# Gate and up projections of a SwiGLU layer as seven block products instead of eight

## The chip, the cores and the metric

The kernel runs on one core of one Trainium2 chip. The metric is the device time of one execution in microseconds (us). Several engines of the core work side by side, each through a queue of its own in order: TensorE (PE, matmuls; its weight loads are listed apart as PEld), VectorE (DVE), ScalarE (ACT), GpSimd (POOL) and SyncE (SP), which issues the transfers.

## The reference

A trunk of two layers on 512 tokens of 1024 features, in float32. Each layer runs a SwiGLU sub-layer, a mixer (convolution and attention) and a second SwiGLU sub-layer, so the program has four SwiGLU stages. The change concerns the first two products of this line:

```python
def _swiglu(h, w_gate, w_up, w_down):
    return (jax.nn.silu(h @ w_gate) * (h @ w_up)) @ w_down
...
h = _rmsnorm(x, norm_g[l, 0]) * (1.0 + mod[:, 0, 1]) + mod[:, 0, 0]
x = x + 0.5 * mod[:, 0, 2] * _swiglu(h, ffn_w_gate[l, 0], ffn_w_up[l, 0], ffn_w_down[l, 0])
```

`h` is 512 x 1024, `w_gate` and `w_up` are 1024 x 2816, `w_down` is 2816 x 1024. The vectors `mod` (shift, scale and gate of each sub-layer) are products of a conditioning vector with a large matrix `ada_w`.

## The kernel before

Activations lie transposed, features on the 128 partitions and the 512 tokens along the row, so a matmul has a 128 x 128 weight block as the loaded operand and up to 512 tokens as the moving one. To keep float32 accuracy each operand is split into a rounded part `hi` and a rest `lo`, and `step` issues three matmuls for one product: hi·hi, hi·lo and lo·hi (lines 216, 217, 218). The two parts of a weight are made on the chip: `Unit.split` has ScalarE cast a piece of 128 x 512 (line 195) and VectorE subtract the cast from the original (line 196). `hh` and `hl` hold the two parts of `h`.

The 2816 hidden features are 22 blocks of 128. `ffn` walks through them in parts of 6, 6, 4, 3 and 3 blocks (`FF_PARTS`). `up` computes for each block m gate and up, 8 feature blocks each, 512 tokens at a time, 48 matmuls in all; `swiglu` then makes silu(gate)·up and splits it (lines 520 to 524). `down_part` multiplies the part's blocks with `w_down` and adds into the residual stream `xT` (line 377). The stages are joined by `boundary`, which ends the old stage with matmuls 256 tokens wide, normalises each half of the tokens as soon as it is there (`modulated`, lines 366 to 371 and 127) and does the first gate and up blocks of the next stage (m = 0 and 1, in the very first stage 0, 1 and 2) with matmuls 256 tokens wide.

Work that is not urgent is woven in: every second `step` calls `tick`, and at a rate of so many steps per tick a generator computes the `mod` vectors on VectorE, mostly with one weighted sum of 128 x 512 a step (line 292), after a transfer of 256 KB each. Such a vector takes 22 steps. Slots for parts (`R`), slots for float32 rows (`F`), four `raw` weight buffers of 128 x 2048 and eight banks of accumulators limit how far the engines run ahead of one another. The order on each engine is set when the program is built.

## Time and profile before

| what | value |
|---|---|
| median of 3 runs | 2733.66 us (2731.41 to 2736.07) |
| profiled execution, device time | 2730.47 us |
| its span, first to last instruction | 2728.5 us |
| TensorE, busy share of the span | 99% |
| VectorE, busy share | 55% |
| ScalarE, busy share | 37% |
| GpSimd, busy share | 11% |

The span lies 2.0 us under the device time of the same execution, and that time 3.2 us under the median. A busy share is an average over all stages; what an edit is worth is read from the stage that it lies in. Matmuls overlap in the profile, so what one costs is read from the distance between starts and not from its own duration.

### The profile page before, as it was taken

How to read it: one execution, taken by the hardware profiler on the slowest of the kernel's cores; microseconds unless marked ns; L12 is line 12 of the kernel's file. 1: busy time of each engine (PE TensorE's matmuls, PEld its weight loads, DVE VectorE, ACT ScalarE, POOL GpSimd, SP SyncE). 2: the span in 40 equal slices, each digit the busy share in tenths (PEclk: the TensorE clock that was granted, in tenths of full speed). 3: DMA queues.
4: the chain of work that ended last, by engine and by line, in shares of the span. 5: the costliest groups of instructions: out<-in, count | busy, mean ns of one | idle time of the engine just before them, and what ended most of it. 6: DMA issues, size and time to landing. Idle time of an engine off the chain costs nothing.

```text
span 2728.5 us, 35693 instructions
## 1 busy us (share of the span) xinstructions
PE 2690.2 (99%) x13489; PEld 2270.8 (83%) x13489; DVE 1513.6 (55%) x2718; ACT 1015.8 (37%) x2106; POOL 294.7 (11%) x887
## 2 busy tenths in 40 slices
PE   6999999999999999999999999999999999999998
PEld 5888789888888888888898888988888888988887
DVE  7955447664563468654485443756646534843434
ACT  4333236344352353332343232443444433532322
POOL 4100014111100020000030000311111000200001
PEclk8999999999999999999999999999999999999999
DMA  8843234342212247433374332333422322532321
GB/s 248 297 149 120 74 122 129 102 132 86 93 62 93 85 148 262 135 99 102 97 233 138 95 108 93 122 90 104 143 74 70 123 78 87 165 108 89 108 70 39
DMA packets 318104, 325.60 MB, mean 119 GB/s; under 512 B 10097, under 2 KB 281836, under 8 KB 317932
## 3 DMA queue, kind: packets, MB, share of 16 engines
q1 hardware_dynamic: 317604, 323.19, 37.1%
q8 instruction: 106, 1.74, 0.3%
q14 instruction: 66, 0.54, 0.1%
q10 hardware_dynamic: 328, 0.13, 0.0%
HBM read 321.15 MB, written 2.13 MB: 118 GB/s over the span
## 4 chain that ended last, share of the span: by engine, by line
PE 95%; DVE 2%; POOL 1%; ACT 1%; DMA 0%; issue 0%; ACTq 0%; DVEq 0%; POOLq 0%
PE mm L216 19%; PE mm L218 19%; PE mm L217 19%; PE o L216 5%; PE o L218 5%; PE o L217 5%; PE at L216 5%; PE at L218 5%; PE at L217 4%; PE mm L886 3%; PE o L733 2%; PE at L624 1%; PE at L626 1%; PE at L625 1%; PE at L400 0%; PE at L709 0%
## 5 line engine op out<-in xcount | busy, mean ns | idle before, releaser
L195 ACT CAST slots_r<-raw 128x512 fp32r<-128x512 f32 (+2 forms) x896 | 522.5, 595 | 1090.6 <-PE mm L217 658.5
L196 DVE TENSOR_TENSOR slots_r<-raw,slots_r 128x512 fp32r<-128x512 f32 (+1 forms) x890 | 573.2, 659 | 588.6 <-ACT slots_r L195 572.0
L216 PE MATMUL mm<-hh,slots_r 128*128 128x512 f32 (+1 forms) x1944 | 732.9, 377 | 0.0
L218 PE MATMUL mm<-hh,slots_r 128*128 128x512 f32 (+1 forms) x1944 | 726.7, 374 | 0.0
L217 PE MATMUL mm<-hl,slots_r 128*128 128x512 f32 (+1 forms) x1944 | 724.9, 373 | 0.0
L218 PEld LDWEIGHTS mm<-hh,slots_r 128*128 128x128 f32 x1944 | 365.2, 188 | 70.3
L217 PEld LDWEIGHTS mm<-hl,slots_r 128*128 128x128 f32 x1944 | 365.9, 188 | 62.4
L216 PEld LDWEIGHTS mm<-hh,slots_r 128*128 128x128 f32 x1944 | 365.9, 188 | 60.7 <-issue 0.6
L216 PE MATMUL mm<-slots_r 128*128 128x512 f32 (+1 forms) x584 | 212.3, 364 | 0.0
L218 PE MATMUL mm<-slots_r 128*128 128x512 f32 (+1 forms) x584 | 211.8, 364 | 0.0
L217 PE MATMUL mm<-slots_r 128*128 128x512 f32 (+1 forms) x584 | 211.8, 363 | 0.0
L292 DVE SCALAR_TENSOR_TENSOR slots_f<-slots_f,cs 128x512 f32<-128x512 f32 (+1 forms) x272 | 191.7, 721 | 18.7 <-DMA slots_f<-in_ada_w_dram 16.5
L391 POOL TENSOR_TENSOR slots_f<-slots_f 128x256 f32<-128x256 f32 x60 | 45.1, 752 | 1053.4 <-ACT slots_f L388 1047.6
L216 PE MATMUL o<-hh,slots_r 128*128 128x512 f32 x344 | 135.5, 394 | 0.0
L218 PE MATMUL o<-hh,slots_r 128*128 128x512 f32 x344 | 134.9, 392 | 0.0
L217 PE MATMUL o<-hl,slots_r 128*128 128x512 f32 x344 | 133.9, 389 | 0.0
L216 PE MATMUL o<-slots_r 128*128 128x512 f32 (+1 forms) x364 | 127.7, 351 | 0.6 <-ACT slots_r L523 0.6
L217 PE MATMUL o<-slots_r 128*128 128x512 f32 (+1 forms) x364 | 126.4, 347 | 0.2 <-DVE slots_r L127 0.2
L218 PE MATMUL o<-slots_r 128*128 128x512 f32 (+1 forms) x364 | 126.5, 348 | 0.0
L216 PE MATMUL at<-hh,slots_r 128*128 128x512 f32 x320 | 125.8, 393 | 0.0
L218 PE MATMUL at<-hh,slots_r 128*128 128x512 f32 x320 | 125.4, 392 | 0.0
L216 PEld LDWEIGHTS mm<-slots_r 128*128 128x128 f32 x584 | 110.2, 189 | 18.1 <-ACT slots_r L195 0.6
(179 smaller groups left out, 3762.8 us busy)
## 6 DMA issues: line engine op xcount, KB each, us to landing
slots_f<-in_ada_w_dram SPq DMA_DIRECT2D x256, 256.0 KB, 3.7
raw<-in_w_in_dram SPq DMA_DIRECT2D x52, 1024.0 KB, 5.1
raw<-in_ffn_w_gate_dram SPq DMA_DIRECT2D x42, 1024.0 KB, 5.3
raw<-in_ffn_w_up_dram SPq DMA_DIRECT2D x42, 1024.0 KB, 5.2
raw<-in_ffn_w_down_dram SPq DMA_DIRECT2D x32, 768.0 KB, 5.5
raw<-in_w_in_dram SPq DMA_DIRECT2D x48, 512.0 KB, 5.2
raw<-in_ffn_w_down_dram SPq DMA_DIRECT2D x20, 512.0 KB, 3.4
slots_f<-in_ada_w_dram SPq DMA_DIRECT2D x16, 512.0 KB, 7.3
```

The costliest lines, as they stand in the source:

```text
L195: A.copy(hv, src)
L196: (eng or V).tensor_tensor(lv, src, f(hv), op=ALU.subtract)
L216: T.matmul(dst, hi, xh[:, cols], start=first, stop=False)
L217: T.matmul(dst, hi, xl[:, cols], start=False, stop=False)
L218: T.matmul(dst, lo, xh[:, cols], start=False, stop=last)
L292: V.scalar_tensor_tensor(acc, w, cs[:, k:k + 1], acc, op0=ALU.mult, op1=ALU.add)
L391: G.tensor_tensor(acc, acc, sq, op=ALU.add)
L624: T.matmul(dst, qh[:, qs], kh[:, :, ks], start=True, stop=False)
L625: T.matmul(dst, qh[:, qs], kl[:, :, ks], start=False, stop=False)
L626: T.matmul(dst, ql[:, qs], kh[:, :, ks], start=False, stop=True)
L733: T.matmul(dst, a, b, start=first[bk], stop=True, skip_group_check=True)
L886: T.matmul(dst, a, b, start=k == 0 and r % 2 == 0 and n == 0, stop=True, skip_group_check=True)
```

## The change

Two blocks (m, m+1) of gate and up are now computed together, as a 2 x 2 product of blocks. The tokens are cut into halves, the 1024 features into halves, and the columns are "256 of gate" and "256 of up". Call the weight blocks a, c (gate, lower and upper features) and b, d (up). Plainly that is eight products of blocks, four for gate and four for up. `seven` forms sums of weight blocks (b-a, d-(b-a), d-b and c-(d-(b-a)), line 585 of the changed kernel), sums of blocks of `h` once per stage (`Sums`, lines 522 to 528), and gets the same four results from seven products (`product`), adding them up in accumulator banks and in float32 slots (lines 581 and 588). Each product takes a weight of 512 x 256 and 256 tokens: 24 matmuls of 256 columns. Its split is one cast and one subtraction of 128 x 1024 each (lines 549 and 146).

Ten pairs a stage go this way, nine in the first, where block 3 is still computed plainly: 39 pairs in the program. The rate of the `mod` steps is multiplied by 0.5 during `up` and by 2.2 during `down_part`. The first product of a pair is put into the pair before. The unsplit `h` is kept in 8 float32 slots (`whole`) until the sums are made; in the first stage it is put together again from its two parts (`rejoined`). `R` grows from 36 to 49 slots, of which 16 hold the sums, `F` shrinks from 25 to 19, and the mixer splits each convolution row where it is made instead of all eight in one place.

```diff
-N_R, N_F, RAWS = 36, 25, 4
+N_R, N_LOW, N_F, RAWS = 49, 33, 19, 4
+SHARE_UP, SHARE_DOWN = 0.5, 2.2
...
-            modulating["due"] += modulating["rate"]
+            modulating["due"] += modulating["rate"] * modulating["share"]
...
+    class Sums:
+        def __init__(self, whole):
+            self.slot = R.at(N_LOW, N_R - N_LOW)
...
+            h11, h21 = whole[:, :4, HALF[0]], whole[:, :4, HALF[1]]
+            h12, h22 = whole[:, 4:, HALF[0]], whole[:, 4:, HALF[1]]
+            V.tensor_tensor(h22, h21, h22, op=ALU.add)
+            self.split(0, h22)
+            V.tensor_tensor(h21, h11, h21, op=ALU.subtract)
+            V.tensor_tensor(h22, h22, h11, op=ALU.subtract)
+            self.split(1, h22)
+            self.split(2, h21)
+            V.tensor_tensor(h22, h12, h22, op=ALU.subtract)
+            self.split(3, h22)
+
+        def split(self, i, src):
+            A.copy(self.hi[:, i], src)
+            sub(self.lo[:, i], src, f(self.hi[:, i]))
...
+    def product(src, x, bank_, first=False):
+
+        hi, lo = R.take(2), R.take(2)
+        hv, lv = (s.ap.rearrange("p (k m) -> p k m", k=4) for s in (hi, lo))
+        A.copy(hv, src)
+        sub(lv, src, f(hv))
+        yield
+        for k in range(4):
+            xh, xl = x(k)
+            for i in range(2):
+                c_ = slice(i * P, (i + 1) * P)
+                dst = bank_[:, HALF[i]]
+                for n, (a, b) in enumerate(((hv[:, k, c_], xh), (hv[:, k, c_], xl), (lv[:, k, c_], xh))):
+                    T.matmul(dst, a, b, start=first and k == i == n == 0, stop=True, skip_group_check=True)
+            if k % 2:
+                tick()
...
+        one = bank("mm")
+        end(run(a, quarter(0, 0), one, True))
+        p1 = kept(one)
+        yield
+        minus(a, b, a)
+        three = bank("o")
+        p = run(a, sums(1), three, True)
+        minus(a, d, a)
+        end(p)
+        end(run(a, sums(2), one))
+        u2 = kept(one)
+        two = bank("at")
+        end(run(c, quarter(1, 0), two, True))
+        plus(p1, two)
+        minus(b, d, b)
+        end(run(b, sums(3), one))
+        u3 = kept(one)
+        plus(u3, three)
+        yield
+        minus(c, c, a)
+        end(run(c, quarter(1, 1), one))
+        end(run(d, sums(4), three))
+        plus(u2, three)
+        done(p1, u2, one, u3)
...
         def up(part):
+            modulating["share"] = SHARE_UP
...
+                pair = ahead.pop(m)
+                next(pair)
+                begin(m + 2)
+                for _ in pair:
+                    pass
...
         def down_part(part):
+            modulating["share"] = SHARE_DOWN
...
                 V.tensor_tensor(conv[m + i].ap, conv[m + i].ap, pd, op=ALU.mult)
+                conv[m + i] = split(conv[m + i])
...
-        zz = [split(s) for s in conv]
+        zz = conv
```

How the order on the engines moves is shown at three places. The first is TensorE inside `up`, far from the edges of a stage. Before, every matmul there runs over 512 columns, into one bank for eight feature blocks:

```order
L216 MATMUL at<-hh,slots_r 128x512
L217 MATMUL at<-hl,slots_r 128x512
L218 MATMUL at<-hh,slots_r 128x512
L216 MATMUL at<-hh,slots_r 128x512
L217 MATMUL at<-hl,slots_r 128x512
L218 MATMUL at<-hh,slots_r 128x512
```

In the changed kernel the same place reads as follows; `o` is the bank called three, `mm` one, `at` two, and 48 matmuls in a row are the last product of a pair and the second of the next:

```order
L558 MATMUL o<-slots_r 128x256 x48
L558 MATMUL mm<-slots_r 128x256 x24
L558 MATMUL at<-hh,slots_r 128x256
L558 MATMUL at<-hl,slots_r 128x256
L558 MATMUL at<-hh,slots_r 128x256 x2
L558 MATMUL at<-hl,slots_r 128x256
```

What moved: 96 matmuls of 512 columns a pair have become 168 of 256, and between two products on the bank `mm` a product on another bank stands.

The second place is VectorE at the start of the second SwiGLU stage (the second one of layer 0), where the sums of blocks of `h` are made. Before, the queue there holds the splits of the first weights, mod steps (L292) and the first two swiglu blocks:

```order
L292 SCALAR_TENSOR_TENSOR slots_f<-slots_f,cs 128x512
L281 TENSOR_TENSOR mod_8222<-dot,vec 128x4
L521 TENSOR_TENSOR slots_f<-slots_f,mm 128x512 x2
L196 TENSOR_TENSOR slots_r<-raw,slots_r 128x512
L127 TENSOR_TENSOR slots_r<-slots_f,slots_r 128x512 x2
L196 TENSOR_TENSOR slots_r<-raw,slots_r 128x512 x3
```

Now, right behind the first two sums (L522, L524), two mod steps and the split of the first product's weight, it holds these (L146 from `raw` is the split of a weight, from `slots_f` 128x1024 that of a sum, L585 a sum of weight blocks, L655 the swiglu of a plain block):

```order
L146 TENSOR_TENSOR slots_r<-slots_f,slots_r 128x1024
L585 TENSOR_TENSOR raw<-raw 128x1024
L525 TENSOR_TENSOR slots_f<-slots_f 128x4x256
L585 TENSOR_TENSOR raw<-raw 128x1024
L146 TENSOR_TENSOR slots_r<-raw,slots_r 128x1024
L146 TENSOR_TENSOR slots_r<-slots_f,slots_r 128x1024 x2
L528 TENSOR_TENSOR slots_f<-slots_f 128x4x256
L655 TENSOR_TENSOR slots_f<-slots_f,mm 128x512 x2
L146 TENSOR_TENSOR slots_r<-slots_f,slots_r 128x1024
L146 TENSOR_TENSOR slots_r<-slots_f,slots_r 128x512 x2
L585 TENSOR_TENSOR raw<-raw 128x1024
L146 TENSOR_TENSOR slots_r<-raw,slots_r 128x1024 x3
```

What moved: the split of the third product's weight (the first of the last three) stands behind sums, splits of sums and the two plain blocks.

The third place is VectorE inside `up`, in the same stage. Before, between two swiglu blocks there are four splits of 128x512 and mod steps:

```order
L196 TENSOR_TENSOR slots_r<-raw,slots_r 128x512 x4
L521 TENSOR_TENSOR slots_f<-slots_f,mm 128x512
L196 TENSOR_TENSOR slots_r<-raw,slots_r 128x512
L127 TENSOR_TENSOR slots_r<-slots_f,slots_r 128x512
L196 TENSOR_TENSOR slots_r<-raw,slots_r 128x512 x2
L521 TENSOR_TENSOR slots_f<-slots_f,at 128x512
```

Now the queue near the end of a pair reads (L588 adds a bank to a kept result, L670 and L666 are the two multiplications of swiglu):

```order
L146 TENSOR_TENSOR slots_r<-raw,slots_r 128x1024 x2
L588 TENSOR_TENSOR slots_f<-slots_f,o 128x512
L585 TENSOR_TENSOR raw<-raw 128x1024 x2
L146 TENSOR_TENSOR slots_r<-raw,slots_r 128x1024 x2
L670 TENSOR_TENSOR slots_f<-slots_f 128x512
L146 TENSOR_TENSOR slots_r<-raw,slots_r 128x1024
L146 TENSOR_TENSOR slots_r<-slots_f,slots_r 128x2x256
L146 TENSOR_TENSOR slots_r<-raw,slots_r 128x1024
L588 TENSOR_TENSOR slots_f<-slots_f,o 128x512
L585 TENSOR_TENSOR raw<-raw 128x1024
L666 TENSOR_TENSOR slots_f<-slots_f 128x512
```

What moved: additions that read a bank (L588) stand in the same queue ahead of splits for products that TensorE will need next.

## Rows read from the trace of the kernel before

**Rows 1.** Head of the page: span, then busy time and share of each engine.

```profile
span 2728.5 us, 35693 instructions
PE 2690.2 (99%) x13489; PEld 2270.8 (83%) x13489; DVE 1513.6 (55%) x2718; ACT 1015.8 (37%) x2106; POOL 294.7 (11%) x887
```

**Rows 2.** Windows: a boundary, then the second SwiGLU stage; busy us, granted clock, DMA.

```profile
1392.00:1396.00 4.00, 4.00 (x38) 4.00 (x37) 4.00 (x10) 2.79 (x6) 1.51 (x2) 1.00 0.91 296
1406.00:1726.00 320.00, 320.00 (x1403) 263.14 (x1402) 160.10 (x264) 98.91 (x175) 13.17 (x48) 1.00 0.38 121
```

**Rows 3.** Timeline of TensorE in that stage, 512 columns: start, duration, line.

```profile
1419.75 0.39 PE L217 MATMUL mm<-hl,slots_r 128*128 128x512 f32 x1
...
1422.04 0.39 PE L218 MATMUL mm<-hh,slots_r 128*128 128x512 f32 x1
```

**Rows 4.** The same view in the boundary ahead of it, 256 columns, and its end.

```profile
1393.78 0.28 PE L218 MATMUL mm<-hh,slots_r 128*128 128x256 f32 x1
...
1395.14 0.28 PE L218 MATMUL mm<-hh,slots_r 128*128 128x256 f32 x1
...
1405.79 0.39 PE L216 MATMUL o<-hh,slots_r 128*128 128x512 f32 x1
```

**Rows 5.** Chain that ended last, a mixer: 192 matmuls of 256 columns.

```profile
663.17 22.62 PE mm L886 x192
```

**Rows 6.** Groups of weight loads in the SwiGLU stage: busy us, mean ns, idle before.

```profile
L216 PEld LDWEIGHTS mm<-hh,slots_r 128*128 128x128 f32 x160 | 30.1, 188 | 6.1
```

**Rows 7.** Groups of VectorE in the SwiGLU stage: busy us, mean ns, idle before.

```profile
L196 DVE TENSOR_TENSOR slots_r<-raw,slots_r 128x512 fp32r<-128x512 f32 x103 | 69.5, 688 | 83.4 <-ACT slots_r L195 81.0 <-PE at L217 2.2
L292 DVE SCALAR_TENSOR_TENSOR slots_f<-slots_f,cs 128x512 f32<-128x512 f32 x32 | 23.3, 748 | 2.6 <-DMA slots_f<-in_ada_w_dram 2.4
L521 DVE TENSOR_TENSOR slots_f<-slots_f,mm 128x512 f32<-128x512 f32 x12 | 8.1, 682 | 8.8 <-PE mm L218 8.8
L521 DVE TENSOR_TENSOR slots_f<-slots_f,at 128x512 f32<-128x512 f32 x10 | 6.9, 686 | 16.9 <-PE at L218 16.9
L196 DVE TENSOR_TENSOR slots_r<-raw,slots_r 128x256 fp32r<-128x256 f32 x16 | 6.5, 419 | 2.2 <-ACT slots_r L195 2.2
```

**Rows 8.** Timeline of VectorE: instructions back to back, merged, with their total time.

```profile
1096.81 0.76 DVE L196 TENSOR_TENSOR slots_r<-raw,slots_r 128x256 fp32r<-128x256 f32 x2
...
1111.87 4.90 DVE L196 TENSOR_TENSOR slots_r<-raw,slots_r 128x512 fp32r<-128x512 f32 x8
```

**Rows 9.** Timeline of VectorE at the start of the second SwiGLU stage.

```profile
1394.99 0.75 DVE L127 TENSOR_TENSOR hl<-slots_f,hh 128x256 fp32r<-128x256 f32 x2
1395.66 0.74 DVE L292 SCALAR_TENSOR_TENSOR slots_f<-slots_f,cs 128x512 f32<-128x512 f32 x1
1396.32 0.68 DVE L196 TENSOR_TENSOR slots_r<-raw,slots_r 128x512 fp32r<-128x512 f32 x1
```

**Rows 10.** Groups of ScalarE: the stage's casts and swiglu, and one of 1024 elements.

```profile
L195 ACT CAST slots_r<-raw 128x512 fp32r<-128x512 f32 x102 | 62.4, 620 | 145.2 <-PE mm L217 63.4 <-PE o L217 36.6 <-PE at L217 24.3
L520 ACT ACTIVATE slots_f<-mm 128x512 f32<-128x512 f32 x11 | 6.6, 597 | 8.4 <-PE mm L218 8.4
L1051 ACT ACTIVATE hl<-slots_f 128x1024 fp32r<-128x1024 f32 x4 | 4.2, 1058 | 2.7 <-DMA slots_f<-in_x_dram 2.7
```

**Rows 11.** DMA: the queue that carries the weights; issues with KB and us to landing.

```profile
q1 hardware_dynamic: 317604, 323.19, 37.1%
...
slots_f<-in_ada_w_dram SPq DMA_DIRECT2D x256, 256.0 KB, 3.7
...
raw<-in_ffn_w_gate_dram SPq DMA_DIRECT2D x42, 1024.0 KB, 5.3
```

More of the change, by code (lines that the diff above doesn't have):

```diff
@@ L76, in __init__, with high, at @@
     def __init__(self, buf, n):
-        self.buf, self.free = buf, list(range(n))
+        self.buf, self.free, self.top = buf, list(range(n)), n
     def take(self, n=1):
         for i in self.free:
-            if all(i + j in self.free for j in range(n)):
-                for j in range(n):
-                    self.free.remove(i + j)
-                return Slot(self, i, n)
+            if i + n <= self.top and all(i + j in self.free for j in range(n)):
+                return self.at(i, n)
         raise ValueError("no slot is free")
+    def high(self):
+        for i in self.free:
+            if i >= self.top:
+                return self.at(i, 1)
+        return self.take()
+    def at(self, i, n):
+        for j in range(n):
+            self.free.remove(i + j)
+        return Slot(self, i, n)
 class Slot:
@@ L94, in give, with apart @@
         self.home.free += range(self.i, self.i + self.n)
+    def apart(self):
+        return [Slot(self.home, self.i + j, 1) for j in range(self.n)]
 @with_exitstack
@@ L416, in __init__ @@
             for m in range(0, NC, 2):
-                mine = [R.take() for _ in range(3)]
+                mine = [R.high() for _ in range(3)]
                 self.slots += mine
@@ new lines, in quarter @@
+    def quarter(part, half):
+        return lambda k: (hh[:, 4 * part + k, HALF[half]], hl[:, 4 * part + k, HALF[half]])
+    def product(src, x, bank_, first=False):
[13 more added lines that the diff above has]
+                tick()
+        hi.give()
+        lo.give()
@@ new lines, in seven, with run, end, kept @@
+    def seven(raw1, raw2, sums, done):
+        a, c = raw1[:, :4], raw1[:, 4:]
+        b, d = raw2[:, :4], raw2[:, 4:]
+        def run(*args):
+            p = product(*args)
+            next(p)
+            return p
+        def end(p):
+            for _ in p:
+                pass
+        def kept(src):
+            s = F.take()
+            A.copy(s.ap, src)
+            return s
+        def minus(dst, x, y):
+            V.tensor_tensor(dst, x, y, op=ALU.subtract)
+        def plus(s, src):
+            V.tensor_tensor(s.ap, s.ap, src, op=ALU.add)
+        one = bank("mm")
[22 more added lines that the diff above has]
+        done(p1, u2, one, u3)
@@ L503, in gate_up, with raws, ffn @@
         held = {}
+        def raws(m):
+            return [load(w[l, i][:, m * P:(m + 2) * P]) for w in (ffn_w_gate, ffn_w_up)]
         def get(m):
             if m not in held:
-                g, u = (halves_of(load(w[l, i][:, m * P:(m + 2) * P]), NC) for w in (ffn_w_gate, ffn_w_up))
+                g, u = (halves_of(raw, NC) for raw in raws(m))
                 held[m], held[m + 1] = (g[0], u[0]), (g[1], u[1])
             return held.pop(m)
-        get.held = held
+        get.held, get.raws = held, raws
         return get
-    def ffn(l, i, get, first):
+    def ffn(l, i, get, first, whole):
         acts = {}
+        R.top = N_LOW
+        sums = Sums(whole.ap.rearrange("p (k n) -> p k n", k=NC))
+        whole.give()
         def swiglu(m, pg, pu):
@@ L810, in mixer @@
         conv = []
+        R.top = N_R
         space = R.take(8)
@@ L815, in mixer, with split @@
             G.memset(f(padded.buf[hs, i]), 0.0)
+        def split(s):
+            hi, lo = R.take(), R.take()
+            A.copy(hi.ap, s.ap)
+            sub(lo.ap, s.ap, f(hi.ap))
+            s.give()
+            return hi, lo
         def deliver(box, n, g, pd):
@@ L929, in gates @@
             return got
-        def split(s):
-            hi, lo = R.take(), R.take()
-            A.copy(hi.ap, s.ap)
-            sub(lo.ap, s.ap, f(hi.ap))
-            s.give()
-            return hi, lo
         y = gates(C_GC, 0)
@@ L1135, in trunk, with rejoined, unsplit @@
     first = list(zip(banks[0::2], banks[1::2]))
+    def rejoined():
+        whole = F.take(8)
+        wv = whole.ap.rearrange("p (k n) -> p k n", k=NC)
+        for k in range(0, NC, 4):
+            V.tensor_tensor(wv[:, k:k + 4], f(hh[:, k:k + 4]), f(hl[:, k:k + 4]), op=ALU.add)
+        return whole
+    def unsplit():
+        whole = F.take(8)
+        return whole, whole.ap.rearrange("p (k n) -> p k n", k=NC)
     rows([ada_b[1].rearrange("(k p) -> k p", p=P)], 72)()
@@ L1150, in trunk @@
         get = gate_up(l, 1)
-        banks = boundary(src, rhs, gate, l, 2, [u for m in range(2) for u in get(m)])
+        whole, wv = unsplit()
+        banks = boundary(src, rhs, gate, l, 2, [u for m in range(2) for u in get(m)], wv)
         give()
@@ L1154, in trunk @@
         modulate((RATE_FFN, modulation(l, 2, 2)), *gens)
-        src, rhs, gate, give = ffn(l, 1, get, [banks[0:2], banks[2:4]])
+        src, rhs, gate, give = ffn(l, 1, get, [banks[0:2], banks[2:4]], whole)
         finish_modulating()
@@ L1158, in trunk @@
             get = gate_up(l + 1, 0)
-            banks = boundary(src, rhs, gate, l + 1, 0, [u for m in range(2) for u in get(m)])
+            whole, wv = unsplit()
+            banks = boundary(src, rhs, gate, l + 1, 0, [u for m in range(2) for u in get(m)], wv)
             give()
```

81 lines of the change are left out of this document (61 added, 20 removed).

## The prediction

> **What bounds the kernel now.** I read the head of the page first: TensorE is busy 99% of the span, VectorE 55%, ScalarE 37% [rows 1]. Then the windows, to see whether that holds inside a SwiGLU stage: in 320 us of the second stage TensorE is busy for all 320.00, at full granted clock (1.00, that is 2.4 GHz), while VectorE works 160.10 us and ScalarE 98.91 [rows 2]. So there is not one gap to remove; only less matmul work helps. In the same stretch VectorE's idle time ends at ScalarE's casts (81.0 us of it), and ScalarE's at matmuls that free slots [rows 7, 10]: both run ahead until the slots are full. The thing to watch is that VectorE has half of its time to spare, and the change spends it.
>
> **What the matmuls give.** Since matmuls overlap, I take the distance between starts. For 512 columns ten steps take 1422.04 - 1419.75 = 2.29 us, 229 ns each [rows 3]. For 256 columns, in the boundary just ahead, twelve take 1395.14 - 1393.78 = 1.36 us, 113.3 ns each [rows 4]. The pattern there is that of the change (hi, hi, lo, each with a weight load of its own), and half the columns cost half the time. In a mixer 192 matmuls of 256 columns take 22.62 us, 117.8 ns each [rows 5]. A pair of blocks was 2 x 48 = 96 matmuls, 96 x 0.229 = 21.98 us. It becomes 7 x 24 = 168, 168 x 0.1133 = 19.03 us, or 19.79 at the slower row. That saves 2.95 us a pair, 115 us over 39 pairs; at 117.8 ns it would be 85.
>
> Weight loads are what could spoil this, for there are 168 in place of 96. A load's record lasts 188 ns [rows 6], more than 113.3, and in the boundary the loads fill 4.00 of 4.00 us [rows 2]; yet starts there stay 113.3 ns apart, so loads overlap each other. The Trainium skill ("TensorE: Matmul & The Clock Gate", section Back-to-back issue gap) says the opposite of a halving: in a real kernel the spacing is set by matmul and weight load together, 81 ns sustained at 128 columns and 131 ns at 512. By the Trainium skill's figures 256 columns would be some 98 ns (an estimate on the line between its two figures), and a pair would go from 12.6 to 16.4 us, 3.8 us longer, so that the change would lose about 150 us. This case's trace disagrees on both the level (229 ns) and the ratio (0.49).
>
> **What VectorE must do for it.** A subtraction of 128 x 512 lasts 688 ns, one of 128 x 256 lasts 419 [rows 7]; back to back, eight of 512 take 4.90 us, hence (4.90 - 0.69) / 7 = 0.60 each, and two of 256 take 0.76, hence 0.34 each [rows 8]. No row shows 1024 elements. The low bound adds 0.26 us per further 256 elements: 0.60 + 2 x 0.26 = 1.12 us. The high bound is two full durations of 512, 1.38. In between, single durations extended give 0.688 + 2 x 0.269 = 1.23. I take 1.12, since VectorE will run densely and dense rows are the nearest.
>
> A pair needs seven splits and four sums of weights of 1024 elements, three additions, two swiglu products and two splits of 512. That is 11 x 1.12 + 7 x 0.60 = 16.5 us; before it was 8 + 2 + 2 of 512, 7.2 us by the same price. Mod steps come on top: 14 ticks at 0.4 x 0.5 make 2.8 steps of about 0.748 us [rows 7], 2.1 us. So VectorE needs 18.6 us in 19.03 us of TensorE: covered, with a margin of 0.4 us where mod steps run and 2.5 where they don't. The Trainium skill ("VectorE: DVE Perf Modes", section Side-by-side) gives one float32 result a cycle and about 150 cycles of start-up for each instruction, hence 1.22 us for 1024 elements (an estimate from the Trainium skill), and a pair would be 19.7 us, more than TensorE's. One instruction alone bears that out (688 ns for 512), but dense rows don't.
>
> A margin of 0.4 doesn't survive idle time. Before, VectorE sat idle for matmuls ahead of the swiglu product 8.8 + 16.9 = 25.7 us in ten pairs, 2.6 us a pair [rows 7]; now the three additions and a product read banks in the same way, with splits for later products queued behind them. Slots let five products be ready ahead (33 low slots, 12 for a part's finished blocks, 4 for a product), so most such waits hide. Between 0 and 2.6 I take half, 1.3 us a pair, so a pair with mod steps takes 18.6 + 1.3 = 19.9 us, 0.87 more than TensorE's. Mod steps outlast `up` differently: the stages must place 97, 88, 66 and 22 steps, and `up` and `down_part` offer about 95, so roughly 9, 9, 7 and 2 pairs run with them: 27 x 0.87 = 23 us lost (0 to 59).
>
> ScalarE casts 1024 in about 1.05 us [rows 10]; seven of them, three copies out of banks, two silu and two casts of 512 (some 0.6 each) are 11.6 us of 19: covered.
>
> **The start of a stage.** The sums of `h` can start when the last half of `h` is written. In the second stage that is at 1395.7, and behind one mod step VectorE is free at 1396.5 [rows 9], while TensorE is busy with the boundary until 1405.8 [rows 4]: 9.3 us of cover. Along the queue of the changed kernel the first product's split ends 4.9 us after that point (three of 1024, two mod steps), the second 5 instructions on at 10.5. The third is ten instructions further on: two splits of sums, L528, two swiglu products, the last sum's split, two splits of 512, a weight sum and itself, 6 x 1.12 + 4 x 0.60 = 9.1 us, and so is ready at 19.6. TensorE wants it after two products of 2.72 us, at 9.3 + 5.4 = 14.7. That is a stall of 4.9 us, say 5. Later splits are then ahead again: the eleventh comes at about 37, wanted at 41. In the first stage block 3 (48 matmuls of 512, 11 us) lies in between, but 4.4 us to put `h` together and 12 or so mod steps forced before the first `down_part` lie against it; I count 5 there too. Four stages: 20 us.
>
> **Small items.** The last pair of a stage has no product of a next pair between the copy of `one` and the next use of that bank: a copy of about 0.6 us [rows 10] and its signals, 1 us, four times 4 us. The copies elsewhere lie beside a product of 2.72 us on another bank. The mod steps moved into `down_part` are 0.88 a tick: part 6 has 24 ticks, 21 steps, 16 us; splits (8 x 0.94) and additions to `xT` (8 x 0.67) are 13 us, together 29 in 144 x 0.229 = 33 us of matmuls: covered, and if not, some of what comes next is late. Their transfers (21 x 256 KB and 8 x 384 KB in 33 us) are some 260 GB/s, where the boundary moved 296 [rows 2]; a load lands after 3.7 to 5.3 us [rows 11], with four ahead. Weights are read once as before. All transfers of weight lie on one hardware queue [rows 11], so the smaller scratch for descriptors costs nothing. The convolution's splits move to places covered by a projection (24 x 0.229 = 5.5 us each); without cover, 16 x 0.69 = 11 us. Fewer `F` slots: 19, of which 8 hold `h` in a boundary; the cover is the same 9.3 us, the cost if gone a few us a boundary.
>
> **The sum.** -115 + 23 + 20 + 4 = -68 us. From the profiled 2730.5 us that is 2662.5; the median of the runs shown lies 3.2 above that execution, so 2666 us.
>
> **The rivals.**
> A, the likeliest, as above: 2666, own range 2640 to 2700. Chance 0.55.
> B, VectorE is hidden throughout: the wait of additions lies beside ready products, and the stage start hardly stalls. Only some 9 us are lost: 2733.7 - 115 + 9 = 2628. For it: half of VectorE is free now. Against it: the third split at the stage's start, whose place is fixed. 0.17.
> C, slower: VectorE becomes the bound of `up`, because an instruction of 1024 costs 1.38 us and nothing overlaps. A pair is then 11 x 1.38 + 7 x 0.69 + 2.1 = 22.1 us against 21.98, so nothing is gained, and the third split comes after 14 x 1.38 + 4 x 0.69 + 2 x 0.75 = 23.6 us, a stall of 8.9 us in each stage: 2733.7 + 39 x 0.1 + 4 x 8.9 = 2773. It decides from the point where a pair takes 19.03 + (115 - 24) / 39 = 21.4 us, an instruction of 1024 of about 1.3 us. For it: every split waits for its cast, as the waits of the stage before show [rows 7]. Against it: the dense rows. 0.13.
> D, half price on wide instructions: 1.23 us each and 0.69 for 512, 18.4 us plus 2.1 plus 1.3 = 21.8 with mod steps, 19.7 without, and a stall of 7 us at each start: 27 x 2.7 + 12 x 0.6 + 28 = 108 us lost, 2727. This is the way in which the change comes to nothing. 0.13.
> E, matmuls of 256 columns are held to the load's 188 ns: 168 x 0.188 = 31.6 us a pair, 39 x 9.6 = 375 us more, 3109. By the Trainium skill's rule above the sign would be the same. Rows 4 show the same pattern at 113.3. 0.02.
>
> **How the numbers follow.** A difference under 0.2% (5.5 us, the spread of the runs) can't be told from none. Faster: A, B and 0.09 of D, 0.81. Same: the rest of D and a crumb of C, 0.05. Slower: 0.14. The range goes from B with nothing lost (2733.7 - 115 = 2619, taken as 2622) to the near end of D, 2725, and leaves out C, E and part of D.
>
> **What would show it.** In the changed profile matmuls of line 558 start 113 to 118 ns apart; 39 pairs take 19 to 21 us each; VectorE is busy over 70% of the span and over 85% in `up`; a gap of 3 to 7 us stands on TensorE behind its first two products in each stage, released by VectorE's split; instructions of 128 x 1024 last about 1.2 us and start about 1.12 apart in dense runs. The prediction is wrong if those cost 1.3 or more, if TensorE waits on VectorE in every pair, or if the mod steps in `down_part` stall it.

## The result and the profile after

The changed kernel takes 2702.41 us (median; 2701.15 to 2703.5) against 2732.53 for the kernel before (2731.12 to 2736.07): a ratio of 0.9888, 95% interval 0.9871 to 0.9905. It is faster, by 1.1% or 30 us where 68 were forecast, and its time lies in the range given. The profiled execution took 2702.5 us.

The head of its page, which answers to [rows 1]:

```profile
span 2700.7 us, 41538 instructions
PE 2632.2 (97%) x16321; PEld 2357.8 (87%) x16321; DVE 1898.2 (70%) x2987; ACT 1167.8 (43%) x2202; POOL 311.2 (12%) x887
```

VectorE rose from 55% to 70%, and TensorE, busy for all of the window 1406 to 1726 us before [rows 2], now idles there for a little. The same window shows how little, and a window inside one pair shows the weight loads (columns as in [rows 2]). The window is called the second stage in [rows 2] and in the prediction; it lies in the third SwiGLU stage, the first of layer 1, since the second ends at 1375 us (see the table under the experiments).

```profile
1406.00:1726.00 320.00, 316.86 (x2233) 296.99 (x2232) 271.15 (x372) 146.87 (x228) 20.31 (x58) 1.00 0.45 143
1300.00:1309.00 9.00, 9.00 (x78) 9.00 (x77) 7.93 (x9) 5.04 (x7) 0.00 (x0) 1.00 0.00 0
```

TensorE is busy for 316.86 of 320 us while VectorE works 271.15, 85%. So VectorE did not become the bound. What the matmuls cost is read from the distances between starts, as in [rows 3, 4]. The timeline of TensorE, first a product on a sum of `h` (24 matmuls merged in a row), then one on `hh` and `hl`:

```profile
1286.69 3.04 PE L558 MATMUL o<-slots_r 128*128 128x256 f32 x24
...
1298.63 0.28 PE L558 MATMUL mm<-hl,slots_r 128*128 128x256 f32 x1
...
1302.17 0.28 PE L558 MATMUL mm<-hl,slots_r 128*128 128x256 f32 x1
```

One matmul lasts 0.28 us, so the 24 start (3.04 - 0.28) / 23 = 120 ns apart. In the other product, on `hh` and `hl`, 30 starts lie between the two rows shown: 3.54 us, 118 ns each. Neither is the 113.3 of [rows 4]. The groups of weight loads in the two kinds of product, answering to [rows 6] (mean ns behind the comma; 1303 to 1309 us, then 1299 to 1301.5):

```profile
L558 PEld LDWEIGHTS o<-slots_r 128*128 128x128 f32 x45 | 5.5, 192 | 0.0
...
L558 PEld LDWEIGHTS mm<-hh,slots_r 128*128 128x128 f32 x15 | 2.3, 188 | 0.0
```

VectorE's groups and one dense run, answering to [rows 7, 8]:

```profile
L146 DVE TENSOR_TENSOR slots_r<-raw,slots_r 128x1024 fp32r<-128x1024 f32 x274 | 328.9, 1217 | 59.6 <-ACT slots_r L549 32.6 <-PE mm L558 8.6 <-PE o L236 8.0
L585 DVE TENSOR_TENSOR raw<-raw 128x1024 f32<-128x1024 f32 x156 | 189.6, 1217 | 1.4
...
1287.56 3.48 DVE L146 TENSOR_TENSOR slots_r<-raw,slots_r 128x1024 fp32r<-128x1024 f32 x3
```

An instruction of 1024 elements lasts 1.217 us alone and starts (3.48 - 1.22) / 2 = 1.13 behind the one before in a dense run. The head of TensorE's waits (us in total, times, longest), and the waits at two places, the first stage and the start of the second:

```profile
PE mm L237 <- DVE slots_r L215: 7.5, 1, 7.5
PE mm L558 <- ACT slots_r L549: 6.8, 6, 1.7
PE mm L558 <- ACT slots_f L581: 6.6, 5, 4.1
...
91.40 0.80 PE L237 MATMUL mm<-hh,slots_r 128*128 128x512 f32 x1 [7.55 <-DVE slots_r L215]
...
1042.77 0.51 PE L558 MATMUL o<-slots_r 128*128 128x256 f32 x2 [0.84 <-ACT slots_r L549]
...
1045.09 1.21 PE L558 MATMUL o<-slots_r 128*128 128x256 f32 x6 [1.58 <-DVE slots_r L146]
...
1054.26 0.50 PE L558 MATMUL mm<-slots_r 128*128 128x256 f32 x2 [1.68 <-ACT slots_r L549]
```

To close the account I read the start of every matmul record of both profiles and split the distances into those of an undisturbed run (the mean of distances of 105 to 135 ns, and of 215 to 250 ns) and what lies over them (waits, and matmuls at the lower clock of 1.2 GHz; ten matmuls of 512 columns that stand ahead of one of 1 or 384 columns are left out in both profiles):

```
                    matmuls   mean ns   sum us     over it us
512 before             9710    229.0
512 after              5966    229.1               22.3 (15.1 before)
256 of L558 after      6576    119.0     782.7     42.1
removed: 3744 x 0.229                    857.4
balance: 782.7 - 857.4 = -74.7;  + 42.1 + 7.2;  the rest of the kernel -2.6: -28.0 (spans: -27.8)
```

### The profile page after: what moved, and what is told of

Same layout as the page of the kernel before. It is cut to its first block, busy times and chain, and to the rows that moved or that the text cites. A ratio compares the mean times of both kernels' runs of the same rounds, so it can differ in the third digit from the quotient of the medians.

```text
span 2700.7 us, 41538 instructions
## 1 busy us (share of the span) xinstructions
PE 2632.2 (97%) x16321; PEld 2357.8 (87%) x16321; DVE 1898.2 (70%) x2987; ACT 1167.8 (43%) x2202; POOL 311.2 (12%) x887
## 4 chain that ended last, share of the span: by engine, by line
PE 76%; DVE 12%; ACT 4%; DMA 3%; issue 2%; POOL 2%; ACTq 0%; SPq 0%; DVEq 0%; POOLq 0%
PE mm L235 12%; PE mm L236 12%; PE mm L558 12%; PE mm L237 12%; PE o L558 6%; DVE slots_r L146 4%; PE mm L1073 3%; PE at L558 3%; PE o L235 2%; PE o L237 2%; PE o L236 2%; DVE slots_f L311 2%; DMA raw<-in_ffn_w_down_dram 2%; PE at L237 2%; PE at L235 2%
## 5 line engine op out<-in xcount | busy, mean ns | idle before, releaser
L215 DVE TENSOR_TENSOR slots_r<-raw,slots_r 128x512 fp32r<-128x512 f32 (+2 forms) x578 | 360.2, 641 | 299.4 <-PE mm L236 155.0
L214 ACT CAST slots_r<-raw 128x512 fp32r<-128x512 f32 (+1 forms) x584 | 323.4, 582 | 411.3 <-PE mm L237 157.3
L237 PE MATMUL mm<-hh,slots_r 128*128 128x512 f32 (+1 forms) x1320 | 482.8, 366 | 7.5 <-DVE slots_r L215 7.5
L235 PE MATMUL mm<-hh,slots_r 128*128 128x512 f32 (+1 forms) x1320 | 487.8, 370 | 0.0
L236 PE MATMUL mm<-hl,slots_r 128*128 128x512 f32 (+1 forms) x1320 | 483.5, 366 | 0.0
L146 DVE TENSOR_TENSOR slots_r<-raw,slots_r 128x1024 fp32r<-128x1024 f32 (+3 forms) x402 | 379.5, 969 | 90.2 <-ACT slots_r L549 32.6
L549 ACT CAST slots_r<-raw 128x1024 fp32r<-128x1024 f32 x274 | 283.4, 1048 | 351.6 <-DVE raw L585 146.9
L558 PE MATMUL mm<-slots_r 128*128 128x256 f32 x1872 | 240.8, 284 | 6.9 <-ACT slots_r L549 5.8
L558 PE MATMUL mm<-hh,slots_r 128*128 128x256 f32 x1264 | 236.7, 283 | 9.1 <-ACT slots_f L581 6.6
L558 PE MATMUL o<-slots_r 128*128 128x256 f32 x1872 | 236.4, 284 | 5.2 <-DVE slots_r L146 3.1
L558 PEld LDWEIGHTS mm<-slots_r 128*128 128x128 f32 x1872 | 230.9, 192 | 9.8 <-ACT slots_r L549 6.8
L558 PEld LDWEIGHTS o<-slots_r 128*128 128x128 f32 x1872 | 229.9, 191 | 8.4 <-DVE slots_r L146 4.2
L558 PEld LDWEIGHTS mm<-hh,slots_r 128*128 128x128 f32 x1264 | 199.1, 190 | 12.7 <-ACT slots_f L581 9.5
L585 DVE TENSOR_TENSOR raw<-raw 128x1024 f32<-128x1024 f32 x156 | 189.6, 1217 | 1.4
L558 PE MATMUL mm<-hl,slots_r 128*128 128x256 f32 x632 | 177.7, 281 | 0.0
```

The source lines that it names most:

```text
L146: V.tensor_tensor(out_, a, b, op=ALU.subtract)
L214: A.copy(hv, src)
L215: (eng or V).tensor_tensor(lv, src, f(hv), op=ALU.subtract)
L235: T.matmul(dst, hi, xh[:, cols], start=first, stop=False)
L236: T.matmul(dst, hi, xl[:, cols], start=False, stop=False)
L237: T.matmul(dst, lo, xh[:, cols], start=False, stop=last)
```

## The experiments

All times are medians; each run is set against the kernel before on the same chip (2731 to 2733 us). Runs whose kernel is edited from the kernel before say so; the others are edits of the changed kernel, 2702.4.

**The price of a matmul, by itself.** In the kernel before, the projections of `up` are issued in halves:

```diff
-                    project([(pg, g)], h, NC)
+                    project_halves(pg, g)
...
+            for i in range(2):
+                for n, (a, b) in enumerate(((hi, hh), (hi, hl), (lo, hh))):
+                    T.matmul(dst[:, HALF[i]], a, b[:, k, HALF[i]], start=k == i == n == 0, stop=True,
+                             skip_group_check=True)
```

> The kernel before with one edit: the gate and up projections of a SwiGLU stage beyond its first blocks (79 blocks, 3792 matmuls of 512 columns) are issued as 7584 matmuls of 256 columns; the work, VectorE and the transfers stay as they were. Theory P (a matmul of 256 columns costs more than half of one of 512, 117.7 to 119.1 ns against 229.5): 7584 x 0.1177 to 0.1191 less 3792 x 0.2295 is 22 to 33 us more, so 2755 to 2766. Rival H (half price, 113.3 ns, the change lost its gain on VectorE): 7584 x 0.1133 less 870 is 11 us less, 2722.

Measured: 2756.5 (1.0093, 1.0078 to 1.0108), 25 us more. Rival H falls: with the same work and VectorE untouched, halving the columns alone loses. Then the same in quarters:

```diff
+            for i in range(4):
+                c_ = slice(i * P, (i + 1) * P)
```

> The kernel before with the same projections issued as 15168 matmuls of 128 columns in place of 3792 of 512. Theory W (a matmul of 256 columns is already at the bound of its weight load, whose record starts 2 to 3 ns behind the matmul before and 110 to 118 ns ahead of its own): 128 columns cost about what 256 do, 109 to 118 ns, so 15168 x 0.109 to 0.118 less 870 is 780 to 920 us more, 3515 to 3650. Rival C (the price is the columns and a fixed part: 229.5 and 117.7 lie on a line of 0.437 ns a column and 6 ns, which gives 62 ns for 128): 15168 x 0.062 less 870 is 70 us more, 2803.

Measured: 3556.6 (1.3019, 1.2993 to 1.3045), 824 us more. The chains that ended last, of the halves and then of the quarters (start, length, count; set them beside [rows 5]):

```profile
1050.06 11.31 PE mm L507 x96
```

```profile
1246.66 21.44 PE mm L508 x192
```

96 matmuls of 256 columns take 11.31 us, 117.8 ns each; 192 of 128 columns take 21.44 us, 111.7 each. Halving the 512 columns about halves the price, halving them again leaves it almost where it is: 229, 117.8, 111.7. Rival C with its 62 ns is out by far. At 256 columns the price is already one of each instruction. In the kernel before, even matmuls of one column (L400) start 112 ns apart in the median. That the weight load sets the price fits the records at 256 columns: loads fill all of the window above, the next load's record starts 2 to 3 ns behind the start of the matmul before, and its own matmul 110 to 118 ns behind that. At 128 columns the records lie otherwise: the load starts 52 ns behind the matmul before and its own matmul 60 ns later (medians). The load itself was not taken away, so that it sets the price is argued and not shown.

**Where the operands lie.** Three runs move tiles in SBUF without touching an instruction.

```diff
-    R = Slots(const.tile([P, N_R, S], F32R, name="slots_r"), N_R)   # e4: the same line, behind hl
+    slots_r = const.tile([P, N_R * S + 16], F32R, name="slots_r")   # e8; + 256 in e12
+            moved = slots_r[:, N_LOW * S + 16:N_R * S + 16]         # the sums' place, e8 and e12
```

> The changed kernel with slots_r behind hl in SBUF, so that hh and hl lie at 57 to 90 KB, the slots for weights at 90 to 157 KB and the sums of h at 157 to 190 KB (before, slots_r lay at 1 to 99 KB, with hh and hl at 157 to 190 KB). If the 119.8 ns of products that read the sums, against 117.7 of those that read hh and hl, come from both operands in one region of addresses, the products on sums come to 117.7 ns: 3744 x 2.1 ns, 8 us less, 2694. If the spacing goes with the tile or with nothing of the place, no change: 2702.

> The changed kernel with the sums of h 64 bytes further on in SBUF, and with them hh and hl (64 bytes of padding behind the slots). Theory L, formed on the run that moved slots_r: the spacing goes with the place of the moving operand against that of the weights, counted modulo 128 bytes. In the changed kernel hh and hl lie 64 bytes off the weights' slots (117.7 ns for 256 columns, 229 to 231 for 512) and the sums lie in line with them (119.8); with slots_r behind hl all were in line, 119.8 ns for 256 and 227 to 228 for 512. Here the sums are off the line and hh and hl on it: products on sums come to 117.7 ns, products on hh and hl to 119.8, matmuls of 512 columns on hh and hl to 227 to 228. Of 3744, 2832 and some 3300 matmuls this is -8, +6 and -8 us: 2690 to 2695. Rival: the spacing goes with the tile, so the sums stay at 119.8 and nothing changes, 2702.

> The changed kernel with only the sums of h 64 bytes further on in SBUF; hh and hl keep their place against the slots (they move by 1024 bytes). From the run before: products on sums come to 117.8 ns for 119.7, the 2832 on hh and hl stay at 117.7, 512 columns stay at 229: 3744 x 1.9 ns, 7 us less, 2695. If the waits take it back, mean 117.8 ns and a time of 2702.

Measured: 2702.1 (0.9892, 0.9877 to 0.9907), 2709.2 (0.9917, 0.9903 to 0.9930) and 2698.4 (0.9877, 0.9863 to 0.9890). The mean spacing of L558 was 119.9, 118.1 and 117.6 ns for 119.0. A product on a sum in the last of them, as above:

```profile
1287.34 2.99 PE L560 MATMUL o<-slots_r 128*128 128x256 f32 x24
...
L560 PEld LDWEIGHTS o<-slots_r 128*128 128x128 f32 x1872 | 226.0, 188 | 9.1 <-DVE slots_r L147 5.2 <-ACT slots_r L551 2.9
```

(2.99 - 0.28) / 23 is 117.8 ns, with loads of 188 ns where there were 120 and 192. So the place of the moving operand against the weights is worth 2 ns, and both go together with the load's length. The first run refuted its own theory of regions (with the sums where `hh` and `hl` had lain, products on them still stood at 120, and those on `hh` and `hl` came to 120 as well). Theory L held for the sums and failed for `hh` and `hl`, which came to 118.7 in place of 119.8, and whose 512-column matmuls went to 232.7 ns in the mean, not down to 227: 128 bytes are not the whole rule.

The place doesn't explain the 113.3 of [rows 4] either, for that spacing comes and goes while `hh` and `hl` stay where they are (which slots held the weights was not read). In the kernel before, 192 matmuls of 256 columns on `hh` and `hl` stand in a row nine times: five boundaries and four mixers. Seven times they start 117.8 ns apart; in one mixer and in the boundary of [rows 4] most of them start 113.3 apart. The chain that ended last shows that mixer, the fast sister of the row in [rows 5] (21.78 / 192 is 113.4 ns):

```profile
465.40 21.78 PE mm L886 x192
```

In the changed kernel the boundary of [rows 4] runs at 117.8, and those ahead of the second and the fourth stage at 113.3. Products reach it too, for a stretch: in e16, one of the runs under the gains below, 344 of them in a row from 1147 us on, among them products on sums ((2.88 - 0.28) / 23 = 113 ns):

```profile
1150.48 2.88 PE L560 MATMUL mm<-slots_r 128*128 128x256 f32 x24
```

About 2% of the changed kernel's product matmuls start 112 to 115 ns apart, and 9% of those in e16. What starts and ends such a stretch was not found.

The order of matmuls in a product, with the three parts outside and the halves inside:

```diff
-            for i in range(2):
-                for n, (a, b) in enumerate(((hv[:, k, c_], xh), (hv[:, k, c_], xl), (lv[:, k, c_], xh))):
+            for n, (w, b) in enumerate(((hv, xh), (hv, xl), (lv, xh))):
+                for i in range(2):
```

> The changed kernel with the matmuls of a product in another order: for each block row and each of the three weight parts the two output halves in turn, in place of the three parts for one half and then the other. Theory P (the spacing of 256-column matmuls is that of the instruction, moved only by where its operands lie): mean 119.0 ns as before, 2702. Rival: the spacing depends on the sequence, such as two loads of the same weights behind each other, or three matmuls into one half of a bank; then the mean moves towards 113 or away, by 6.6 us for each ns.

Measured: 2697.6 (0.9873, 0.9859 to 0.9886); mean spacing 119.0, so the sequence is not it. What moved were the waits over it, 33.1 us for 42.1; they were read from an execution of 2693.3 us, and the interval of the time overlaps the changed kernel's, so a gain is not shown.

**VectorE's load.** First, less of it, by leaving work out:

```diff
         def minus(dst, x, y):
-            V.tensor_tensor(dst, x, y, op=ALU.subtract)
+            pass
         def plus(s, src):
-            V.tensor_tensor(s.ap, s.ap, src, op=ALU.add)
+            pass
```

> The changed kernel with VectorE relieved: the four sums of weights and the three additions of each pair are left out (the products run on the unsummed weights, and their additions are missing). That takes 4 x 1.2 + 3 x 0.65, some 6.8 us a pair, off VectorE. Theory P (the gain was lost on the price of 256 columns): 6552 x 5.8 ns, 38 us, stay lost, and only the waits of some 42 us can go, most of those that VectorE causes: 2665 to 2690, never below 2655. Rival V (the gain was lost on VectorE): the time falls to the full gain, 2618 to 2630.

Measured: 2684.1 (0.9826, 0.9810 to 0.9843), 18 us less; mean spacing 119.0, over it 27.5 us for 42.1. Rival V falls: with a third of a pair's VectorE work gone, the time is still 54 us above the upper end of what it forecast. Then the mod steps' old pace:

```diff
-SHARE_UP, SHARE_DOWN = 0.5, 2.2
+SHARE_UP, SHARE_DOWN = 1.0, 1.0
```

> The changed kernel with the mod steps at their old pace in both halves of a stage (shares 1.0 and 1.0 for 0.5 and 2.2). A pair that runs beside mod steps then asks 2.1 us more of VectorE (5.6 steps of 0.75 us for 2.8). If VectorE has no margin in a pair, some 13 of the 27 such pairs become about 2 us longer: 2715 to 2730. If the waits that are left have other causes (the order of a pair's casts and copies, the start of a stage), the time stays within 5 us of 2702.

Measured: 2703.0 (0.9897, 0.9883 to 0.9911): no difference, so 2 us more of VectorE's time in a pair with mod steps cost nothing that shows. Last, two ways to hand VectorE's work to GpSimd:

```diff
-                weighted(acc, w.ap, k)                       # e9, the mod steps
+                    A.mul(w.ap, w.ap, cs[:, k:k + 1])
+                    G.tensor_tensor(acc, acc, w.ap, op=ALU.add)
-        minus(b, d, b)                                       # e10, the third sum of weights
+        minus_pool(b, d, b)                                  # G.tensor_tensor, after the second sum
```

> The changed kernel with the mod steps taken off VectorE: each row block is multiplied on ScalarE and added on GpSimd. VectorE loses some 255 instructions of 0.75 us, 191 us, nearly all inside the SwiGLU stages. The run without the sums of weights and additions took 265 us off VectorE and gained 18 us; at that rate this gains 13: 2689. If the waits come from the order of a pair's own instructions and not from VectorE's load, no change. If ScalarE's 0.6 us more a step delay the casts, or GpSimd's additions slow VectorE's instructions down, slower: 2705 to 2720.

> The changed kernel with one of a pair's four sums of weights on GpSimd, the third, whose operands are ready early and which is wanted by the fifth product only. VectorE loses 39 x 1.22 us, 48 us: by the rate of 18 us in 265, 3 us less, 2699. If GpSimd, which takes 1.4 to 1.7 us for 512 elements and so some 3 for these, comes too late for the split behind it, slower by up to 10.

Measured: 2830.8 (1.0355, 1.0341 to 1.0370) and 2751.7 (1.0071, 1.0058 to 1.0084); both far beyond the rivals' figures. TensorE's and ScalarE's longest waits in the first, then two groups of the second:

```profile
PE mm L562 <- ACT slots_f L585: 33.2, 11, 8.3
...
ACT slots_f L352 <- DMA slots_f<-in_ada_w_dram: 139.1, 78, 7.2
```

```profile
L588 POOL TENSOR_TENSOR raw<-raw 128x1024 f32<-128x1024 f32 x39 | 105.7, 2710 | 683.9 <-DVE raw L585 615.5 <-issue 33.9 <-ACT slots_f L581 19.4
...
L146 DVE TENSOR_TENSOR slots_r<-raw,slots_r 128x1024 fp32r<-128x1024 f32 x274 | 353.9, 1309 | 77.5 <-ACT slots_r L549 46.9 <-PE mm L558 10.7 <-PE o L236 8.0
```

In the first, ScalarE's multiplication (L352) waits 139 us for its rows from memory, and casts and copies wait behind it in the queue: TensorE then waits 33 us for the copy alone. VectorE, freed of 191 us of mod steps, is busy only 57 us less (1841.7 for 1898.2), so its other instructions grew longer beside GpSimd's additions. In the second, 39 sums of 2.71 us raise the mean of VectorE's own splits from 1217 to 1309 ns. The mean hides what happens: 249 of the 274 splits last 1.22 us as before, and the 25 that overlap a sum last 2.43 us in the median. Two splits in a row, clear of a sum and then behind the start of one:

```profile
1072.12 2.35 DVE L146 TENSOR_TENSOR slots_r<-raw,slots_r 128x1024 fp32r<-128x1024 f32 x2
...
1075.69 2.41 POOL L588 TENSOR_TENSOR raw<-raw 128x1024 f32<-128x1024 f32 x1 [19.43 <-DVE raw L585]
...
1076.13 4.19 DVE L146 TENSOR_TENSOR slots_r<-raw,slots_r 128x1024 fp32r<-128x1024 f32 x2
```

The sum ends at 1078.1; the first split, begun at 1076.13, lasts until 1079.2, about one split's length behind that end. Sharing out the work lost more than VectorE's load cost.

**The first stage and the order of a pair.** Three edits of what TensorE waits for, each with a clear target (e2, e6 and e7):

```diff
-                    if m % 2:                               # e2
+                    if m % 2 and m + 1 >= len(first):
+        for pair in get.held.values():                      # e6, ahead of sums = Sums(...)
+            for u in pair:
+                u.split()
+        two = bank("at")                                    # e7, moved up behind the first product
+        end(run(c, quarter(1, 0), two, True))
+        plus(p1, two)
```

> The changed kernel without the first product of a pair that the first stage starts and never uses (24 matmuls, one cast, one split, two loads of 1 MB). If the 7.8 us stall at 83.6 us and the half clock behind it are its doing, 8 to 15 us less: 2688 to 2694. If they come from the sums of h and the mod steps that stand ahead on VectorE, only the 24 matmuls go: about 3 us less, 2699.

> The changed kernel, with the weights of block 3 of the first stage split before the sums of h are made (they stand behind them now). If the 7.8 us stall at 83.6 us is the splits of block 3 queued on VectorE behind the sums, it goes, and the half clock behind it too (some 12 matmuls at 427 ns in place of 229, 2.4 us): 8 to 10 us less, 2692 to 2695, unless the sums are late in turn for the next product, which gives part of it back. If the stall comes from the mod steps that are forced there, no change.

> The changed kernel with another order of a pair's seven products: the one on the lower half of the gate weights and the lower first quarter of h, which needs no sum, comes second and not fourth. At the start of the second to fourth stage VectorE then has 2.85 us more for the first split of a sum of weights and of h: if the stall there is VectorE's queue, 2 to 4 us less in each of the three stages, 6 to 12 less, 2690 to 2696. If the queue is only moved (its split stands ahead of the sums now), no change; if the later products of a pair lose what the first ones gain, slower by as much.

Measured: 2710.0 (0.9921, 0.9906 to 0.9935), 2712.7 (0.9929, 0.9917 to 0.9942) and 2724.4 (0.9976, 0.9966 to 0.9986): all slower than the changed kernel. Why e7 is slower was not followed. In e2 the wait for L215 stayed, 7.1 us. In e6 it went, and the sums came late in turn:

```profile
98.37 0.50 PE L558 MATMUL o<-slots_r 128*128 128x256 f32 x2 [1.69 <-ACT slots_r L549]
99.70 0.51 PE L558 MATMUL o<-slots_r 128*128 128x256 f32 x2 [0.82 <-DVE slots_r L146]
```

The start of the broadcast that ends each part (L378), read from each profile, tells where the rest went (us; the last two kernels belong to the next part):

```
                     stage 1  mixer 1  stage 2  stage 3  mixer 2  last matmul
changed                413.3   1013.6   1374.9   1727.2   2327.7    2693.9
e2_no_waste            405.4   1006.8   1377.0   1734.7   2334.3    2700.5
e6_split_first         411.0   1010.0   1379.4   1733.2   2336.1    2704.2
e7_c_second            418.5   1021.1   1388.0   1740.8   2341.4    2715.4
e17_sorted             412.4   1013.6   1382.7   1735.9   2337.6    2704.6
e18_sorted_no_waste    406.8   1008.4   1372.4   1726.5   2329.2    2697.6
```

e2 gains 7.9 us in the first stage and loses 8.9 in the second (1377.0 - 1006.8 for 1374.9 - 1013.6) and 5.4 in the third, whose instructions are the same; in the whole profile L558 into `mm` waits 12.0 us for VectorE's splits (L146), where it waited 2.3.

**What carries it over.** A stage inherits the lists of free slots from what ran before. With both lists sorted at its start:

```diff
         R.top = N_LOW
+        R.free.sort()
+        F.free.sort()
```

> The changed kernel with the lists of free slots sorted at the start of each SwiGLU stage, so that the slots which a stage takes no longer depend on what was taken before it. If the order of the slots carries the waits from stage to stage, this moves the time by some 5 to 15 us either way (2688 to 2717), most of it in the second to fourth stage. If not: 2702.

> The same, and without the product that is never used. Alone that edit ended the first stage 8 us earlier and lost 15 us in the second and third stage. If the slots' order was the cause of that loss, it doesn't come with sorted slots: 8 us less than the run with sorted slots alone. If the banks' turn or the times at which mod steps and loads meet the stage are the cause, the loss comes again: 5 to 10 us more.

Measured: 2713.4 (0.9926, 0.9912 to 0.9939) without and 2705.0 (0.9900, 0.9886 to 0.9913) with e2's edit. With the same slots at each stage's start the edit keeps its gain, 8.4 us (the two intervals just touch), and the second stage does not lose it (364.0 us against 369.1). So the order of the slots decides over some 10 us of waits, and the changed kernel's own order is by luck the better of the two tried: sorting alone costs 11. That the slots decide through later reuse is the natural reading, but which reuse was not followed.

**A version of the gains.** Three kernels join edits shown above: the order of matmuls and the place of the sums (e11 and e12); these and the guard of e2; these and the shares of e5.

> The changed kernel with the two edits that gained a little alone: the halves of a product in turn for each weight part (4.8 us less than the changed kernel's 2702.4), and the sums of h 64 bytes further on (4.0 less). If they add up: 2693 to 2695. If both only shuffled the waits: 2698 to 2704.

> The same two edits, and without the product that is never used. Alone that cost 7.5 us, all of it in waits of the second and third stage, while the first stage ended 8 us earlier. If these waits belong to that order of the banks and slots by chance, 8 less than the run with two edits: 2685 to 2687. If they belong to the edit, 2700 to 2705.

> The two edits with the mod steps at their old pace, 1.0 and 1.0. Alone the pace made no difference (2703.0). If VectorE has margin enough in a pair, as that run says: the same as with the two edits, 2693 to 2698. If the shorter products (117.6 ns for 119) leave VectorE too little: 2700 to 2710.

Measured: 2697.5 (0.9874, 0.9859 to 0.9889), 2703.0 (0.9894, 0.9881 to 0.9909) and 2700.7 (0.9882, 0.9866 to 0.9899). The spacing came down as it should (117.4 to 117.7), yet the gains do not add up, and no interval lies clear of the changed kernel's. I call none of them faster than it.

## Why the prediction was wrong in size

The sign, the bound and most mechanisms held; the step that failed is the price of a 256-column matmul. Term by term:

- **"half the columns cost half the time"**: this step failed. It took 113.3 ns from one boundary [rows 4], and that was the rare price: two of nine like stretches of the same trace run at it for the most part, the other seven at 117.8. L558 came to 119.0, and over 6552 used matmuls that is 37 us, nearly all of the 38 us missed: 30 us lie between 113.3 and 117.8, and 8 come from the products on sums at 119.9. The row beside it, 117.8 [rows 5], was the usual one: its saving of 85 was written down as the other end and not used. The matmuls saved 74.7 us where 115 stood; 2.9 of that gap are the 24 unused matmuls. e1 shows without the change that 256 columns cost more than half of 512, and e13 that at 256 the columns hardly set the price any more.
- **"so loads overlap each other"**: true, and not the point. A load with its matmul still follows the one before at 111.7 ns even with 128 columns (e13). Rival E pointed at the right place with the wrong size: not the load's 188 ns, but a floor near 112. The Trainium skill ("TensorE: Matmul & The Clock Gate", section Back-to-back issue gap) says that matmul and load together set the spacing; the records at 256 columns fit that without showing it, while its figures (81 and 131 ns, 98 estimated at 256 columns) stand against 111.7, 229 and 119.0 here.
- **VectorE's price**: right. 1.217 us alone and 1.13 dense for 1024 elements, where 1.12 was taken; C and D, which built on 1.38 and 1.23, fall.
- **The waits, 20 + 23 + 4 = 47 us**: measured 42.1 + 7.2 = 49.3. Of this the starts of the stages make some 21 (second 4.1 in waits and some 1.3 at half clock; third 1.3, fourth 3.5; first 0.85 + 7.55 and 13 matmuls at half clock, 2.6), where 20 stood. That the sums agree is in part luck: the first stage lost 11 where 5 stood, and the third, for whose start (1396 to 1406 us) the 4.9 were worked out under the name of the second, lost 1.3. In the first it is not the third split but block 3's weights behind the sums. Waits for the copies (L581), 4 us in the forecast, make 6.6, of which 4.1 stand once in the middle of the first stage's `up`.
- **The 23 us of pairs with mod steps**: right in size by luck, for its reason is not borne out. What is left of the waits, some 28 us, is near 23 + 4; but with the mod steps at double their pace in `up` nothing changed (e5); taking 265 us off VectorE gained 18 (e3). e17 and e18 show that the order of the slots has a part in the waits; which wait goes back to which reuse stays open.
- **Unseen**: the first stage starts a pair that it already has, 24 matmuls and 2 MB of loads. Reading how `begin` is called for the first blocks would have shown it. Its worth is 8 us in e18 against e17; without the sorting, leaving it out cost 7.5 (e2).

Of the signs listed: VectorE at 70% and 85%, right; spacing 113 to 118, wrong; 19 to 21 us a pair, at its upper edge (168 x 0.119 is 20.0, and 21.1 with its share of the 42.1 us); a gap of 3 to 7 us behind the first two products, smaller and in pieces; that TensorE would not wait on VectorE in every pair, right.

## What to carry to other kernels

Before trading long matmuls for more short ones, price the short one in every stretch of the trace that has it, and take the usual or the dearest price: here 256 columns stood at 113, 118 and 120 ns in one trace, and only the rarest of the three made the trade look like half price. An algorithm that saves an eighth of the products can lose a good part of it to the instruction's fixed price, and the trade can be priced without the algorithm, by issuing the old work in short matmuls. In a kernel this tight an edit that clearly removes a wait may move others through the order of its buffers, so judge it stage by stage and not by the total alone.

## What the hardware showed unexpectedly

- A matmul on the split parts (float32r in the program) started every 229, 117.8 and 111.7 ns at 512, 256 and 128 columns, at full granted clock.
- The same 256-column matmuls on `hh` and `hl`, which don't move, run 117.8 ns apart in most stretches and 113.3 in some. The boundary of [rows 4] was of the second kind in the kernel before and of the first in the changed one. Why stays open: the loads of that boundary last 188 ns as in the runs at 117.8, as this group of the kernel before (1392 to 1396 us) shows.

```profile
L217 PEld LDWEIGHTS mm<-hl,slots_r 128*128 128x128 f32 x13 | 2.4, 188 | 0.0
```

- The place of the operands in SBUF changed the spacing by 2 ns at 256 columns (119.9 to 117.6 over the layouts tried), together with the load's length (192 and 188 ns), and at 512 columns on `hh` and `hl` from 228.1 (e4) to 232.7 (e8).
- A VectorE split of 128 x 1024 that overlapped a GpSimd sum of the same size lasted 2.43 us in the median, for 1.22 clear of one (e10).
- The clock fell behind waits, to 1.2 GHz: two windows of the changed kernel, behind the wait of 7.55 us and behind the first two at the second stage's start (the column ahead of the DMA share is the granted clock):

```profile
91.40:96.80 5.40, 5.40 (x13) 4.24 (x14) 5.40 (x8) 0.00 (x0) 0.00 (x0) 0.50 0.48 147
...
1046.00:1049.00 3.00, 3.00 (x16) 3.00 (x16) 3.00 (x5) 1.76 (x3) 0.00 (x0) 0.50 0.23 44
```
